# Chunked linear attention without POOL: one query product, copied by ScalarE into the block-diagonal tile; splits of the earliest norm on VectorE

## The chip, the core and the metric

The kernel runs on one core of a Trainium2 chip. The metric is the time of one execution on the device in microseconds (us), as the median of several runs. The engines are TensorE (PE in the profile; PEld is its weight load), VectorE (DVE), ScalarE (ACT), GpSimd (POOL) and SyncE (SP), which here only issues transfers.

## The reference

Two layers of a transformer block work on 512 latent tokens and 256 context tokens of width 1024. Each layer is: half a SwiGLU feed-forward step, a token mixer with three head groups (gated linear attention, windowed attention, differential attention) that share an input and an output projection, and a second half feed-forward step, all with modulated RMS norms. In the last layer the context tokens only serve as keys. The part that the change touches is the gated linear attention, in chunks, forwards and backwards:

```python
def step(state, inp):
    kc, vc, gc = inp[0], inp[1], inp[2]
    cum = jnp.cumsum(gc, axis=2)
    last = cum[:, :, -1:, :]
    new_state = (jnp.exp(last[:, :, 0, :, None]) * state
                 + jnp.einsum('bhjd,bhjv->bhdv', kc * jnp.exp(last - cum), vc))
    qc = inp[3]
    o_inter = jnp.einsum('bhid,bhdv->bhiv', qc * jnp.exp(cum), state)
    decay = jnp.exp(jnp.where(causal, cum[:, :, :, None, :] - cum[:, :, None, :, :], -jnp.inf))
    att = jnp.einsum('bhid,bhjd,bhijd->bhij', qc, kc, decay)
    return new_state, o_inter + jnp.einsum('bhij,bhjv->bhiv', att, vc)
```

All is float32; the kernel keeps that accuracy by splitting each operand of a large product into a high and a low part and adding three products.

## The kernel before

Activations lie transposed, features on the partitions and tokens along the columns. A large product is three TensorE instructions (`mm3`, lines 405 to 407). The high part of an operand is a rounded copy by ScalarE (`split`, line 369), the low part a subtraction on VectorE or POOL (line 370). Weights come in by transfers that SyncE issues.

`gla_mix` (line 1302) is the linear attention after its projections. For each direction it makes the cumulated log gates (lines 1334, 1336), the keys scaled to the end of each chunk (1346 to 1348), the states chunk by chunk (1361 to 1368) and the scaled queries for the states (1375, 1376). Within a chunk of 128 it doesn't form the decay for each pair of tokens, but goes through seven levels of block size s = 64, 32, 16, 8, 4, 2, 1. At each level and for each direction `d`, the queries of one half of a block of 2s tokens meet the keys of the other half. This takes, for one level-direction:

- line 1417: the cumulated gates minus those of the middle of each block, into `E` (128 partitions x n tokens);
- lines 1418, 1419: two exponentials of half of `E` each, on ScalarE;
- line 1423: the keys times their half of `E`;
- lines 1424 to 1427: for each of the four heads (32 partitions each) the queries times their half of `E`, written into the head's own columns of `qbd`, a tile that is zero elsewhere, so that one TensorE product yields all four heads apart (block-diagonal);
- lines 1439, 1444 or 1450: the TensorE products of keys and `qbd`;
- lines 1454 to 1469: the results go into the attention tile, by copies for s of 64 and 32, by predicated copies on VectorE for the rest.

`E`, `qbd` and the keys have three buffers each that rotate from one level-direction to the next. n is 512 for the latent tokens and 256 for the context; layer 0 does both, layer 1 the first alone, so there are 14 + 14 + 14 level-directions.

This work doesn't run alone. The tail of the windowed attention (lines 1198 to 1248), the output projection of the other two head groups (lines 405 to 407 with 1534, whose operands are split by lines 369 and 370) and the modulation of later stages (lines 274 to 331) are traced between its steps. The order of the instructions on each engine is fixed when the program is built, by a scheduler that may move an instruction ahead of earlier ones of the trace. An engine works through its queue in that order.

The table `CFG` (line 86) names the engine of each piece of work by a letter: V for VectorE, P for POOL, A for ScalarE. `GK` stands for lines 1348, 1376 and 1417, `KV` for line 1423, `Q` for the four heads of line 1427, `HS` for the low parts of the first feed-forward weights, that come in two halves (`half_split`, line 865, called at lines 1668 and following), `NA` for the norms: a letter per feature block, d for a fused low part on VectorE (line 461), s or S for a `split` of the finished value, whose low part is on POOL for s and on VectorE for S (line 458).

At the start, the norm of the first feed-forward step (`norm_x`, line 1660) is made in two halves of four feature blocks, as the modulation of each half is ready, and the first products of that step begin with the first half. Lines 711 to 729 (`t_prep`) then prepare sums of the normed blocks on VectorE for the later products.

Of the kernel before, what the change touches and what calls it, by code (L numbers as in the profile page):

```python
# [15 lines left out]
ALU = mybir.AluOpType  # L16
# [66 lines left out]
    return rope, mats, masks  # L83


CFG = dict(big=('VVVV', 'PPPP', 'VVVV', 'VVVV', 'VV'), small=('VPVV', 'PPPP', 'VVVV', 'VVPP', 'VV'), T=['VVVVVVVVVVVV', 'VVVVVVVVVVVV', 'VVVVVVVVVVVV', 'VVVVVVVVVVVV'], QW=['PVVV', 'VVVV', 'VVVV', 'VVVV'], QS=['VVVV', 'VVVV', 'VVVV', 'VVVV'], TS1=[0, 4, 0, 0], TS2=[0, 4, 0, 0], NA=['dsdsdsds', 'dsdsdsds', 'dsdsdsds', 'dsdsdsds', 'dsdsdsds', 'dsdsdsds'], RS='V', PS=['V', 'V', 'V', 'V'], PL=['V', 'V', 'V', 'V'], ORD='1c6u2eA5dxA37yfAg4hA', ORD1='1c236ueA5dxgA7yfA4hA', ORD2='1c236ueA5dxgA7yfA4hA', SPLIT=0.9, E0=18, E1=16, SA=10, SB=3, F0=(2, 14), F1=(0, 6), Q='PVVV', KV='P', OL='V', DM='sbsbsbsb', G3=2, N0=0, QB='bbbs', HS=['PPPP', 'PPPP'], LO='VV', RM='V', GK='PPP', DC='AAVV', SC='VAVAV', VE='AA', GC='VVA', ST='qxdrmlsnMSN', XS='AVAVAV', XE='VAVAVAVAVAVA', PB=['s', 'bb', 's', 'bb'])


@with_exitstack
def hybrid_kernel(ctx: ExitStack, tc: tile.TileContext, x, c, ctx_in, c_ctx, w_mod, b_mod, g_ffn1, w_ffn1_in,  # L90
# [3 lines left out]
    nc = tc.nc  # L94
# [8 lines left out]
    P = cpool.tile([128, 3840], F32, name="P")  # L103
# [47 lines left out]
    ENG = {"P": nc.gpsimd, "V": nc.vector}  # L151
# [15 lines left out]
    def copy(e, dst, src):  # L167
        if e == "A":
            nc.scalar.activation(dst, src, AF.Copy)
        else:  # L170
            ENG[e].tensor_copy(dst, src)
# [75 lines left out]
    def sum_x(a):  # L247

        sq = P[:, (a % 3) * 1024:(a % 3 + 1) * 1024]
        if CFG["XS"][a] == "V":  # L250
            nc.vector.scalar_tensor_tensor(sq, xin[a], 1.0, xin[a], op0=ALU.mult, op1=ALU.mult, accum_out=ss0[:, a:a + 1])
# [3 lines left out]
    def load_x():  # L255
        bank = cyc(gtile, atile, btile_, atile, stile, stile)

        for k in range(NK):
            ps = bank()
            for a in range(4):  # L260
                nc.tensor.transpose(ps[:, a * 128:(a + 1) * 128], xin[a][:, k * 128:(k + 1) * 128], ident)
            copy(CFG["XE"][k], xT[:, k, :SEQ], ps[:, :SEQ])
        for k in range(0, NK, 2):
            ps = bank()
            for b in range(4):
                nc.tensor.transpose(ps[:, b * 128:(b + 1) * 128], xin[4 + b % 2][:, (k + b // 2) * 128:(k + b // 2 + 1) * 128], ident)
            copy(CFG["XE"][NK + k // 2], xT[:, k:k + 2, SEQ:], ps[:, :512].rearrange("p (k t) -> p k t", k=2))

# [174 lines left out]
    def norm_apply(l, which, piece, pb, ks):  # L443
# [4 lines left out]
        for k in ks:  # L448
# [4 lines left out]
            sh = mod[l][:, si, k, t:t + 1]  # L453
            mode = CFG["NA"][3 * l + which][k]
            if mode in "sS":
# [65 lines left out]
    def ffn(l, which, w_i, w_o, pieces, side=None):  # L521
# [3 lines left out]
        beside = side() if side else iter(())  # L525
        ME, LE, WE, SE, UE = CFG["big" if pieces[-1][1] > SEQ else "small"]
        last = ((0, 256), (256, 512), CP) if CP in pieces else pieces
# [20 lines left out]
        def quad_stages(first=False):  # L548
            we, se = (CFG["QW"][fi], CFG["QS"][fi]) if first else (WE, SE)

# [751 lines left out]
    def gla_mix(l, cq):  # L1302
# [38 lines left out]
        for d in range(2):  # L1341
# [17 lines left out]
            for i, cc in enumerate(order):  # L1359
# [3 lines left out]
                for h in range(4):  # L1363
                    pr, vs = slice(32 * h, 32 * h + 32), slice(64 * h, 64 * h + 64)
# [16 lines left out]
        for t0, t1 in ((XP, CP) if cq else (XP,)):  # L1381
# [6 lines left out]
            for hf in range(2):  # L1388
                m = n // 2
                qbd = qbd_reg[rr[0] % 3].rearrange("p (h t) -> p h t", h=4)[:, :, :m]  # L1390
                rr[0] += 1
                for h in range(4):
                    pr = slice(32 * h, 32 * h + 32)
# [11 lines left out]
            for li, s in enumerate(LEVELS):  # L1405
                nb = n // (2 * s)
                ops = []
                for d in range(2):
                    cu = cum[d][:, t0:t1].rearrange("p (b t) -> p b t", t=2 * s)
                    mid = cu[:, :, s - 1:s] if d == 0 else cu[:, :, s:s + 1]  # L1410
                    E = e_reg[rr[0] % 3][:, :n].rearrange("p (b t) -> p b t", t=2 * s)
                    qbd = qbd_reg[rr[0] % 3].rearrange("p (h t) -> p h t", h=4)[:, :, :n // 2]
                    kt_ = kt_reg[rr[0] % 3][:, :n]
                    rr[0] += 1
                    iq = slice(s, 2 * s) if d == 0 else slice(0, s)
                    jk = slice(0, s) if d == 0 else slice(s, 2 * s)
                    ENG[CFG["GK"][2]].tensor_tensor(E, cu, mid.to_broadcast([128, nb, 2 * s]), op=ALU.subtract)
                    act(E[:, :, iq], E[:, :, iq], AF.Exp, scale=TAU)
                    act(E[:, :, jk], E[:, :, jk], AF.Exp, scale=-TAU)
                    q3 = g_q[:, t0:t1].rearrange("p (b t) -> p b t", t=2 * s)  # L1420
                    k3 = g_k[:, t0:t1].rearrange("p (b t) -> p b t", t=2 * s)
                    kv3 = kt_.rearrange("p (b t) -> p b t", t=2 * s)
                    ENG[CFG["KV"]].tensor_tensor(kv3[:, :, jk], k3[:, :, jk], E[:, :, jk], op=ALU.mult)
                    for h in range(4):
                        pr = slice(32 * h, 32 * h + 32)
                        eng = ENG[CFG["Q"][h]]
                        eng.tensor_tensor(qbd[pr, h].rearrange("p (b t) -> p b t", t=s), q3[pr, :, iq], E[pr, :, iq], op=ALU.mult)
                    ops.append((qbd, kt_))
                for r0 in (range(0, ncn, 2) if s == 64 else (0,)):
                    rn = 2 if s == 64 else ncn  # L1430
                    pl = btile()
                    for d in range(2):
                        qbd, kt_ = ops[d]
                        for cc in range(r0, r0 + rn):
                            kc = kt_[:, cc * 128:(cc + 1) * 128]
                            cl = cc - r0
                            if s == 64:
                                po = 64 * d
                                nc.tensor.matmul(pl[po:po + 64, cl * 256:(cl + 1) * 256], kc[:, po:po + 64],
                                                 qbd[:, :, cc * 64:(cc + 1) * 64], start=True, stop=True)  # L1440
                            elif s == 32:
                                for b in range(2):
                                    po = 64 * b + 32 * d
                                    nc.tensor.matmul(pl[po:po + 32, cc * 128:(cc + 1) * 128], kc[:, po:po + 32],
                                                     qbd[:, :, cc * 64 + 32 * b:cc * 64 + 32 * b + 32],
                                                     start=True, stop=True)
                            else:
                                co = d * n // 2 + cc * 64
                                for g in range(4):
                                    nc.tensor.matmul(pl[32 * g:32 * g + 32, co:co + 64], kc[:, 32 * g:32 * g + 32],  # L1450
                                                     qbd[:, :, cc * 64 + 16 * g:cc * 64 + 16 * g + 16], start=True, stop=True)
                    if s == 64:
                        p4 = pl[:, :rn * 256].rearrange("p (c h i) -> p c h i", c=rn, h=4)
                        nc.scalar.copy(att[0:64, r0:r0 + rn, :, 64:128], p4[0:64])
                        nc.vector.tensor_copy(att[64:128, r0:r0 + rn, :, 0:64], p4[64:128])
                    elif s == 32:
                        p4 = pl[:, :n].rearrange("p (c h i) -> p c h i", c=ncn, h=4)
                        for g in range(4):
                            pr = slice(32 * g, 32 * g + 32)
                            io = 32 * (g ^ 1)  # L1460
                            (nc.scalar.copy if g % 2 else nc.vector.tensor_copy)(att[pr, :, :, io:io + 32], p4[pr])
                    else:
                        for d in range(2):
                            io = s if d == 0 else 0
                            a = li - 2
                            mk = masks[:, (5 * d + a) * 16:(5 * d + a + 1) * 16]
                            src = pl[:, d * n // 2:(d + 1) * n // 2]
                            dst = dg.rearrange("p c h i -> p (c h) i").rearrange("p a (b t) -> p a b t", t=2 * s)[:, :, :, io:io + s]
                            nc.vector.copy_predicated(
                                dst, mk.rearrange("p (b t) -> p b t", t=s).unsqueeze(1).to_broadcast([128, ncn * 4, 16 // s, s]),  # L1470
                                src.rearrange("p (a b t) -> p a b t", b=16 // s, t=s))
                yield
            for g in range(4):
                pr = slice(32 * g, 32 * g + 32)
# [26 lines left out]
    SPLIT = CFG["SPLIT"]  # L1501
# [116 lines left out]
    G3 = CFG["G3"]  # L1618
# [147 lines left out]
```

## Time and profile before

| | |
|---|---|
| runs, us | 2964.78, 2964.88, 2969.39; median 2964.88 |
| profiled execution, us | 2966.68 |
| its span, first to last instruction, us | 2964.9 |
| granted TensorE clock, mean | 0.991 |
| PE busy, us | 2857.1 |
| DVE busy, us | 2215.8 |
| ACT busy, us | 1222.6 |
| POOL busy, us | 455.5 |

The busy times are sums over instructions of one engine; engines run side by side, so they don't add up to the span. A line of the profile names the source line of the instruction (L1427), its engine, its operation, the tile written and the tiles read, the shape as partitions x columns, and the number of instructions. A share of the clock of 1.00 is 2.4 GHz, half of it 1.2 GHz. The tile names H, W1, W2, FA, FB, A2, G, B and so on are areas that hold different things at different stages; f or r behind them is the type.

### The profile page before, as it was taken

How to read it: one execution, taken by the hardware profiler on the slowest of the kernel's cores; microseconds unless marked ns; L12 is line 12 of the kernel's file. 1: busy time of each engine (PE TensorE's matmuls, PEld its weight loads, DVE VectorE, ACT ScalarE, POOL GpSimd, SP SyncE). 2: the span in 40 equal slices, each digit the busy share in tenths (PEclk: the TensorE clock that was granted, in tenths of full speed). 3: DMA queues.
4: the chain of work that ended last, by engine and by line, in shares of the span. 5: the costliest groups of instructions: out<-in, count | busy, mean ns of one | idle time of the engine just before them, and what ended most of it. 6: DMA issues, size and time to landing. Idle time of an engine off the chain costs nothing. (4 is left out here: it accounts for less than half of the span.)

```text
span 2964.9 us, 48602 instructions
## 1 busy us (share of the span) xinstructions
PE 2857.1 (96%) x19464; PEld 2499.0 (84%) x19464; DVE 2215.8 (75%) x3925; ACT 1222.6 (41%) x2310; POOL 455.5 (15%) x440
## 2 busy tenths in 40 slices
PE   7899999999999889999999999999999999899998
PEld 5798999888776568999999899999988766689898
DVE  6777787655668878878776787777664678799996
ACT  4333333345455435333333542333354555354443
POOL 3001011110002431101010101101010013123432
PEclk9999999999999999999999999999999999999999
DMA  6332312223445341221212122212222343223332
GB/s 219 114 121 86 93 58 88 68 54 92 100 127 171 101 128 30 85 71 57 86 58 72 44 72 70 73 60 69 72 66 70 77 134 100 72 79 116 91 106 87
DMA packets 314245, 262.38 MB, mean 88 GB/s; under 512 B 27528, under 2 KB 290340, under 8 KB 314020
## 3 DMA queue, kind: packets, MB, share of 16 engines
q1 hardware_dynamic: 311712, 255.47, 29.1%
q10 hardware_dynamic: 2308, 3.82, 0.4%
q8 instruction: 153, 2.51, 0.3%
q14 instruction: 72, 0.59, 0.1%
HBM read 247.72 MB, written 2.10 MB: 84 GB/s over the span
## 5 line engine op out<-in xcount | busy, mean ns | idle before, releaser
L369 ACT ACTIVATE W0r<-R 128x1024 fp32r<-128x1024 f32 (+2 forms) x229 | 219.6, 965 | 353.5 <-PE a L407 78.3
L370 DVE TENSOR_TENSOR W0r<-R,W0r 128x1024 fp32r<-128x1024 f32 (+1 forms) x193 | 215.8, 1123 | 61.8 <-ACT W0r L369 37.4
L369 ACT ACTIVATE W1r<-R 128x1024 fp32r<-128x1024 f32 (+1 forms) x149 | 141.7, 953 | 250.1 <-PE a L406 74.5
L825 DVE SCALAR_TENSOR_TENSOR X<-s,dmod,X 128x512 f32<-128x512 f32 x252 | 150.5, 627 | 65.9 <-PE s L407 65.9
L370 POOL TENSOR_TENSOR FAr<-P,FAr 128x384 fp32r<-128x384 f32 (+1 forms) x64 | 75.7, 1187 | 566.8 <-ACT FAr L369 533.9
L370 POOL TENSOR_TENSOR FBr<-P,FBr 128x384 fp32r<-128x384 f32 (+1 forms) x60 | 72.4, 1208 | 582.2 <-ACT FBr L369 480.9
L405 PE MATMUL g<-Hr,W0r 128*128 128x384 f32 (+3 forms) x400 | 140.3, 351 | 9.5 <-ACT P L163 9.3
L163 ACT ACTIVATE P<-s,sm 128x768 f32<-128x768 f32 (+3 forms) x160 | 119.0, 750 | 60.4 <-DVE sm L1061 38.5
L406 PE MATMUL g<-Hr,W0r 128*128 128x384 f32 (+3 forms) x400 | 136.7, 342 | 0.2 <-POOL Hr L370 0.2
L370 DVE TENSOR_TENSOR W1r<-R,W1r 128x1024 fp32r<-128x1024 f32 (+1 forms) x102 | 109.3, 1078 | 26.3 <-ACT W1r L369 12.8
L825 DVE SCALAR_TENSOR_TENSOR X<-a,dmod,X 128x256 f32<-128x256 f32 (+1 forms) x170 | 101.9, 600 | 30.4 <-PE a L407 30.2
L407 PE MATMUL g<-Hr,W0r 128*128 128x512 f32 (+3 forms) x324 | 112.4, 347 | 1.1 <-DVE W0r L370 1.1
L556 DVE TENSOR_TENSOR P<-R 128x512 f32<-128x512 f32 x80 | 58.0, 725 | 65.2 <-DMA R<-in_w_ffn_in_dram 65.2
L407 PE MATMUL a<-Hr,W0r 128*128 128x384 f32 (+2 forms) x332 | 106.7, 321 | 0.0
L1061 DVE TENSOR_REDUCE sm<-s 128x1 f32<-128x768 f32 (+1 forms) x80 | 65.8, 844 | 41.3 <-PE s L1060 41.2
L405 PEld LDWEIGHTS g<-Hr,W0r 128*128 128x128 f32 (+1 forms) x400 | 74.4, 186 | 23.8 <-ACT P L163 9.5
L370 POOL TENSOR_TENSOR Hr<-P,Hr 128x256 fp32r<-128x256 f32 (+1 forms) x64 | 55.1, 862 | 254.4 <-ACT Hr L369 253.6
L405 PE MATMUL a<-Hr,W0r 128*128 128x384 f32 (+2 forms) x280 | 91.8, 328 | 0.4 <-DVE ms L330 0.4
L406 PE MATMUL a<-Hr,W0r 128*128 128x384 f32 (+2 forms) x280 | 90.9, 325 | 0.0
L369 ACT ACTIVATE FAr<-P 128x384 fp32r<-128x384 f32 (+2 forms) x80 | 39.8, 498 | 113.2 <-DVE P L769 83.5
L405 PE MATMUL s<-Hr,W0r 128*128 128x384 f32 (+2 forms) x240 | 81.5, 340 | 5.0 <-ACT Hr L460 4.8
L405 PE MATMUL b<-Hr,W0r 128*128 128x384 f32 (+3 forms) x248 | 82.8, 334 | 1.0 <-DVE sm L1208 0.5
(853 smaller groups left out, 10167.9 us busy)
## 6 DMA issues: line engine op xcount, KB each, us to landing
R<-in_w_ffn_in_dram SPq DMA_DIRECT2D x164, 512.0 KB, 4.4
R<-in_w_mod_dram SPq DMA_DIRECT2D x104, 512.0 KB, 4.4
R<-in_w_ffn_out_dram SPq DMA_DIRECT2D x40, 1024.0 KB, 4.9
R<-in_w_in_dram SPq DMA_DIRECT2D x28, 512.0 KB, 4.0
W2f<-in_w_mod_dram SPq DMA_DIRECT2D x24, 512.0 KB, 3.6
R<-in_w_ffn_in_dram SPq DMA_DIRECT2D x6, 1024.0 KB, 5.1
Gr<-Bf SPq DMA_DIRECT2D x48, 96.0 KB, 2.2
Hf<-in_w_mod_dram SPq DMA_DIRECT2D x4, 1024.0 KB, 13.4
```

Source lines behind the costliest of these rows:

```text
L163: i = nc.scalar.activation(dst, src, func, **kw).ins
L369: nc.scalar.activation(dst_hi, src, AF.Copy)
L370: (lo_eng or nc.vector).tensor_tensor(dst_lo, src, dst_hi.bitcast(F32), op=ALU.subtract)
L405: nc.tensor.matmul(ps, wh, rh, start=first, stop=False)
L406: nc.tensor.matmul(ps, wh, rl, start=False, stop=False)
L407: nc.tensor.matmul(ps, wl, rh, start=False, stop=last)
L556: ENG[se[0]].tensor_tensor(SB[:, 0:512], a21, a22, op=ALU.add)
L825: nc.vector.scalar_tensor_tensor(xT[:, m, p0:p1], p_, dmod[l][:, 3 + which, m, t:t + 1], xT[:, m, p0:p1], op0=ALU.mult, op1=ALU.add)
L1061: nc.vector.tensor_reduce(sm[:, s:s + 1], S[:, k0:TOK], AX.X, ALU.max, negate=True)
```

## The change

The four per-head query products of each level-direction become one product over all 128 partitions, in place in `E`, on VectorE. Its four parts are then copied into the block-diagonal tile, by ScalarE for all four heads (`QC='AAAA'`). The subtraction of line 1417, the key products and the products of lines 1348 and 1376 go from POOL to VectorE. So do the low parts of the first weights (`HS`, two times four splits of 128x512) and those of the odd feature blocks of the very first norm (`NA[0]`: four blocks of 512 and four of 256 tokens). The zero fills of lines 1378 and 1379 stay on POOL, and so does POOL's work elsewhere.

```diff
-CFG = dict(..., NA=['dsdsdsds', 'dsdsdsds', ...], ..., Q='PVVV', KV='P', ..., HS=['PPPP', 'PPPP'], ..., GK='PPP', ...)
+CFG = dict(..., NA=['dSdSdSdS', 'dsdsdsds', ...], ..., QC='AAAA', KV='V', ..., HS=['VVVV', 'VVVV'], ..., GK='VVV', ...)
@@ -1421,10 +1421,10 @@
                     k3 = g_k[:, t0:t1].rearrange("p (b t) -> p b t", t=2 * s)
                     kv3 = kt_.rearrange("p (b t) -> p b t", t=2 * s)
                     ENG[CFG["KV"]].tensor_tensor(kv3[:, :, jk], k3[:, :, jk], E[:, :, jk], op=ALU.mult)
+                    nc.vector.tensor_tensor(E[:, :, iq], q3[:, :, iq], E[:, :, iq], op=ALU.mult)
                     for h in range(4):
                         pr = slice(32 * h, 32 * h + 32)
-                        eng = ENG[CFG["Q"][h]]
-                        eng.tensor_tensor(qbd[pr, h].rearrange("p (b t) -> p b t", t=s), q3[pr, :, iq], E[pr, :, iq], op=ALU.mult)
+                        copy(CFG["QC"][h], qbd[pr, h].rearrange("p (b t) -> p b t", t=s), E[pr, :, iq])
                     ops.append((qbd, kt_))
```

## Rows read from the trace of the kernel before

**Rows 1.** The page, busy us, share of the span and instructions of an engine.
```profile
PE 2857.1 (96%) x19464; PEld 2499.0 (84%) x19464; DVE 2215.8 (75%) x3925; ACT 1222.6 (41%) x2310; POOL 455.5 (15%) x440
```
**Rows 2.** Busy us by stretch; columns: length, PE, PEld, DVE, ACT, POOL, clock, DMA.
```profile
890.00:910.00 20.00, 15.86 (x136) 9.45 (x133) 17.24 (x38) 13.21 (x37) 11.24 (x12) 0.91 0.44 136
960.00:1030.00 70.00, 57.00 (x760) 39.01 (x758) 64.37 (x134) 34.90 (x85) 33.30 (x35) 0.98 0.37 114
1040.00:1090.00 50.00, 42.06 (x443) 28.37 (x440) 40.28 (x95) 16.51 (x49) 24.49 (x42) 0.97 0.37 109
2480.00:2550.00 70.00, 55.92 (x698) 38.57 (x696) 64.61 (x115) 28.54 (x64) 32.21 (x35) 0.93 0.35 95
sum 210.00, PE 170.84 PEld 115.40 DVE 186.50 ACT 93.17 POOL 101.24; mean PE 42.71 PEld 28.85 DVE 46.63 ACT 23.29 POOL 25.31
```
**Rows 3.** Waits of PE, whole span: who waited for whom, us, times, longest.
```profile
PE g L1450 <- DVE Hf L1427: 10.9, 6, 3.2
...
PE s L1450 <- DVE Hf L1427: 2.6, 3, 1.4
...
PE g L1450 <- POOL FBf L1417: 1.7, 1, 1.7
```
**Rows 4.** Timeline of DVE: start us, us, line, shape, count (merged where back to back).
```profile
906.65 1.75 DVE L1204 SCALAR_TENSOR_TENSOR sm<-sm,nsink 128x2 f32<-128x2 f32 x1
...
986.55 1.28 DVE L1427 TENSOR_TENSOR Hf<-W1f,Hf 32x256 f32<-32x256 f32 x3
...
1001.95 4.31 DVE L1427 TENSOR_TENSOR Hf<-W1f,Hf 32x256 f32<-32x256 f32 x3
```
**Rows 5.** Groups of DVE, shapes apart, line 1427: count, busy us, mean ns, idle before.
```profile
L1427 DVE TENSOR_TENSOR Hf<-W1f,Hf 32x256 f32<-32x256 f32 x54 | 38.4, 712 | 2.2 <-PE g L1399 0.7 <-ACT Hf L163 0.3
L1427 DVE TENSOR_TENSOR FBf<-W1f,FBf 32x256 f32<-32x256 f32 x30 | 17.4, 580 | 1.0 <-ACT FBf L163 0.3
L1427 DVE TENSOR_TENSOR Hf<-W1f,Hf 32x128 f32<-32x128 f32 x30 | 12.2, 407 | 2.0 <-ACT Hf L163 1.4
L1427 DVE TENSOR_TENSOR FBf<-W1f,FBf 32x128 f32<-32x128 f32 x12 | 5.5, 459 | 0.3
```
**Rows 6.** Groups of DVE, two-input instructions little disturbed; last, one of the timeline.
```profile
L1496 DVE TENSOR_TENSOR Hf<-Hf,s 128x512 f32<-128x512 f32 x4 | 2.7, 687 | 4.1 <-PE s L985 4.1
...
L1248 DVE TENSOR_TENSOR FAf<-FAf,a 128x256 f32<-128x256 f32 x4 | 1.6, 410 | 0.5 <-PE a L1244 0.5
...
L1330 DVE TENSOR_TENSOR Hf<-Hf 128x768 f32<-128x768 f32 x4 | 3.8, 950 | 0.0
...
1058.09 0.28 DVE L1427 TENSOR_TENSOR Hf<-W1f,Hf 32x128 f32<-32x128 f32 x1
```
**Rows 7.** Groups of ACT, shapes apart: block-diagonal copies of line 1394, exponentials.
```profile
L163 ACT ACTIVATE Hf<-Hf 128x256 f32<-128x256 f32 x36 | 13.3, 415 | 28.6 <-POOL Hf L1417 28.6
...
L1394 ACT ACTIVATE Hf<-W1f 32x256 f32<-32x256 f32 x16 | 6.6, 411 | 1.2 <-POOL Hf L1378 1.0
...
L1394 ACT ACTIVATE Hf<-W1f 32x128 f32<-32x128 f32 x4 | 1.2, 308 | 0.7 <-PE s L1450 0.6
```
**Rows 8.** Timeline of PE: one kind of product, before and inside the slow clock.
```profile
2505.38 0.40 PE L407 MATMUL a<-A2r,W0r 128*128 128x512 f32 x1
...
2513.97 0.63 PE L407 MATMUL a<-A2r,W0r 128*128 128x512 f32 x1
```
**Rows 9.** Timelines of DVE and PE at the start of the kernel.
```profile
35.58 2.94 DVE L450 SCALAR_TENSOR_TENSOR P<-X,dmod,KLf 128x256 f32<-128x256 f32 x2
...
38.45 1.75 DVE L461 SCALAR_TENSOR_TENSOR Hr<-P,mod,Hr 128x512 fp32r<-128x512 f32 x1
...
50.65 0.69 DVE L284 TENSOR_TENSOR Bf<-Bf,a 128x512 f32<-128x512 f32 x1 [5.04 <-PE a L274]
...
57.69 3.75 DVE L450 SCALAR_TENSOR_TENSOR P<-X,dmod,KLf 128x256 f32<-128x256 f32 x4
...
87.83 0.69 PE L405 MATMUL g<-Hr,W0r 128*128 128x384 f32 x1 [9.29 <-ACT P L163]
```

More of the change, by code (lines that the diff above doesn't have):

```diff
@@ L83, in _shape_constants @@
     return rope, mats, masks
-CFG = dict(big=('VVVV', 'PPPP', 'VVVV', 'VVVV', 'VV'), small=('VPVV', 'PPPP', 'VVVV', 'VVPP', 'VV'), T=['VVVVVVVVVVVV', 'VVVVVVVVVVVV', 'VVVVVVVVVVVV', 'VVVVVVVVVVVV'], QW=['PVVV', 'VVVV', 'VVVV', 'VVVV'], QS=['VVVV', 'VVVV', 'VVVV', 'VVVV'], TS1=[0, 4, 0, 0], TS2=[0, 4, 0, 0], NA=['dsdsdsds', 'dsdsdsds', 'dsdsdsds', 'dsdsdsds', 'dsdsdsds', 'dsdsdsds'], RS='V', PS=['V', 'V', 'V', 'V'], PL=['V', 'V', 'V', 'V'], ORD='1c6u2eA5dxA37yfAg4hA', ORD1='1c236ueA5dxgA7yfA4hA', ORD2='1c236ueA5dxgA7yfA4hA', SPLIT=0.9, E0=18, E1=16, SA=10, SB=3, F0=(2, 14), F1=(0, 6), Q='PVVV', KV='P', OL='V', DM='sbsbsbsb', G3=2, N0=0, QB='bbbs', HS=['PPPP', 'PPPP'], LO='VV', RM='V', GK='PPP', DC='AAVV', SC='VAVAV', VE='AA', GC='VVA', ST='qxdrmlsnMSN', XS='AVAVAV', XE='VAVAVAVAVAVA', PB=['s', 'bb', 's', 'bb'])
+CFG = dict(big=('VVVV', 'PPPP', 'VVVV', 'VVVV', 'VV'), small=('VPVV', 'PPPP', 'VVVV', 'VVPP', 'VV'), T=['VVVVVVVVVVVV', 'VVVVVVVVVVVV', 'VVVVVVVVVVVV', 'VVVVVVVVVVVV'], QW=['PVVV', 'VVVV', 'VVVV', 'VVVV'], QS=['VVVV', 'VVVV', 'VVVV', 'VVVV'], TS1=[0, 4, 0, 0], TS2=[0, 4, 0, 0], NA=['dSdSdSdS', 'dsdsdsds', 'dsdsdsds', 'dsdsdsds', 'dsdsdsds', 'dsdsdsds'], RS='V', PS=['V', 'V', 'V', 'V'], PL=['V', 'V', 'V', 'V'], ORD='1c6u2eA5dxA37yfAg4hA', ORD1='1c236ueA5dxgA7yfA4hA', ORD2='1c236ueA5dxgA7yfA4hA', SPLIT=0.9, E0=18, E1=16, SA=10, SB=3, F0=(2, 14), F1=(0, 6), QC='AAAA', KV='V', OL='V', DM='sbsbsbsb', G3=2, N0=0, QB='bbbs', HS=['VVVV', 'VVVV'], LO='VV', RM='V', GK='VVV', DC='AAVV', SC='VAVAV', VE='AA', GC='VVA', ST='qxdrmlsnMSN', XS='AVAVAV', XE='VAVAVAVAVAVA', PB=['s', 'bb', 's', 'bb'])
 @with_exitstack
```

## The prediction, made before the change was run

> **What bounds the kernel now.** I read the page first: TensorE holds 96% of the span, VectorE 75% [rows 1]. A kernel so full can only gain where TensorE stands still, so the next view is busy time by stretch. Four stretches hold all the linear-attention work that the change touches: 890 to 910 us and 960 to 1030 us (layer 0, the 512 latent tokens), 1040 to 1090 us (layer 0, the 256 context tokens), 2480 to 2550 us (layer 1). Of their 210 us TensorE is busy 170.8, idle 39.2; VectorE is busy 186.5, and in the second and fourth about 92% of the time; ScalarE is busy 93.2, less than half; POOL 101.2 [rows 2]. So in these stretches, and in few others, VectorE is the engine that sets the pace.
>
> Who ends TensorE's waits says the same: the products of line 1427 on VectorE and the POOL subtraction of line 1417 end 15.2 us of them in the three longest groups [rows 3]; the rest is spread over many short waits on other VectorE work in the same queue.
>
> Third, what makes VectorE so busy. Three of its 32x256 products take 1.28 us when POOL does nothing, and 4.31 us while POOL runs its own share of the same level; a 128x2 product, that has next to nothing to do, took 1.75 us beside POOL's 128x768 product [rows 4]. The two engines disturb each other, so a VectorE instruction can cost over three times its price while POOL is busy.
>
> **The change, part by part.** I make the sum against the profiled execution, 2966.68 us with a span of 2964.9; the median of the three runs, 2964.88, is 1.8 us lower, and the last step takes that off.
>
> Linear attention on VectorE. There are 28 level-directions of 512 tokens (14 in each layer) and 14 of 256. Before, each gives VectorE three products of 32 partitions: 126 in all, 73.5 us [rows 5]. Alone they would take 84 x 0.43 (a third of the 1.28 us in rows 4) and 42 x 0.28 [rows 6], together 47.9 us, so some 26 us of it is stretch from POOL. After, each direction gives VectorE a subtraction, a key product and a query product over 128 partitions: 0.69 + 0.41 + 0.41 us at 512 tokens, 0.41 + 0.28 + 0.28 at 256 [rows 6] (a product costs by its columns, not by its partitions, so the 32x128 row stands for 128x128). That is 28 x 1.51 + 14 x 0.97 = 55.9 us. Line 1348 adds four products of 128x768 and line 1376 two of 128x768 and two of 128x512: 6 x 0.95 + 2 x 0.69 = 7.1 us [rows 6]. VectorE so gives up 73.5 and takes 63.0: 10.5 us less, although it does all of POOL's work. The other VectorE instructions of these stretches (186.5 - 73.5 = 113 us) lose their stretch too. I can't see how much; I put it at 10 us, a stretch of 9% where line 1427 had over 50%, with ends at 0 and 26. VectorE is then relieved of 20.5 us (10.5 to 36).
>
> How much of that TensorE sees: 39.2 us of idle time is there to be had, and VectorE is nearly the only candidate in two of the four stretches, less so in the context stretch where it is busy 40.3 of 50 us. I take two thirds of the relief: **14 us less**, with ends at 0 (another engine is late in its place) and 30.
>
> The query copies on ScalarE. 28 x 4 copies of 32x256 at 0.41 us and 14 x 4 of 32x128 at 0.31 [rows 7] (line 1394 does this very kind of copy into the same tile) are 63.3 us more on ScalarE. Its cover is its own idle time, 210 - 93.2 = 117 us in these stretches, and the exponentials of the 512-token levels alone wait 28.6 us for POOL's subtraction [rows 7]. With the copies it stands at 156 of 210 us. I cost them at nothing; without that cover they cost up to 63.3 us. They bring one new wait: a copy must wait until TensorE has read its block-diagonal buffer three directions before, a wait that VectorE and POOL had. Behind it on ScalarE stand the next direction's exponentials, the weight and activation splits of line 369 for the output projection, and PSUM evacuations, and TensorE waits for all of these. The chain of one direction gets no shorter by itself: 0.69 (subtract) + 0.83 (two exponentials) + 0.41 (product) + 1.64 (four copies) = 3.6 us after; before, the last two steps were 3 x 0.43 = 1.3 us undisturbed, and 4.3 us as the third of rows 4. The gain is the stretch, not fewer steps.
>
> TensorE's clock. The granted clock was 0.91, 0.98, 0.97 and 0.93 in the four stretches [rows 2]: after gaps TensorE is held at 1.2 GHz for a while, where a 128x512 product takes 0.63 us and not 0.40 [rows 8]. The means lose 1.8 + 1.4 + 1.5 + 4.9 = 9.6 us of full clock. Fewer gaps give part back: **2 us less**, ends 0 and 6.
>
> The earliest norm and the first weight splits. Eight 128x512 weight splits and four 128x512 plus four 128x256 norm splits go to VectorE: 12 x 0.69 + 4 x 0.41 = 9.9 us. Four of the weight splits fall where VectorE idles 5.04 us before line 284 [rows 9] and cost nothing. The other 7.1 us lie on a queue that the timeline shows packed up to 91 us, and whose end ends the 9.29 us wait of TensorE at 87.8 us (through ScalarE's SiLU, which stands behind splits of VectorE's sums in its queue) [rows 9]. Against them the stretch goes: two 128x256 products that took 2.94 us, one 128x512 that took 1.75 and four 128x256 that took 3.75 should take 0.82, 0.69 and 1.64 [rows 6, 9], 5.3 us less, and there are smaller ones. I take **1 us more**, ends -1 and +7. If a split of a weight is late, TensorE's third product of that k waits for it (line 407), and all behind it.
>
> POOL keeps the feed-forward splits and the norm splits of the later layers, so all else stays as it is. The scheduler orders each engine's queue anew when instructions change engine, which may move a few us anywhere; I add 3 us to both ends for it.
>
> **The sum**: 2966.7 - 14 - 2 + 1 = 2951.7, and 1.8 less on the scale of the median: about 2950.
>
> **The rivals.**
> (a) *Turned into another wait.* The chain per direction stays at 3.6 us, the copies wait for TensorE, and TensorE's waits end on ScalarE where they ended on VectorE. For: the 15.2 us of rows 3 all hang on that chain. Against: VectorE's own queue, not the chain, is full in two of the four stretches. Relief of 0 to 3 us, time 2959 to 2970, say 2964.
> (b) *ScalarE becomes the bound: slower.* Per level of 512 tokens it has eight copies (3.3 us), four exponentials (1.66 us) and its evacuations, over 5 us in one queue in order, while the swa exponentials and line 369 stand in the same queue. It decides once more than 15 of the 63.3 us, a quarter, stand ahead of something that TensorE waits for; if a half does, the time is 2965 + 32 - 15 = 2982. Against: ScalarE's 117 us of idle time. The Trainium skill ("ScalarE: Activation LUTs", Rules for kernel authors) sends plain elementwise work to VectorE and not to ScalarE; by that rule this rival would be the outcome, and no run so far shows it.
> (c) *More than forecast.* If POOL and VectorE exclude each other for whole instructions, VectorE gets back far more than I put down, up to the 36 us end, and the idle of 39.2 us all but goes: 30 us for the gaps and 4 for the clock, 2965 - 34 = 2931. The rows with 4.31 and 1.75 us speak for it; that many stretched instructions are only slightly stretched speaks against. The Trainium skill ("SBUF — State Buffer", SBUF: two separate sides) says just this: a shared port pair is locked for the whole instruction between a VectorE instruction with two SBUF inputs and a GpSimd one that reads SBUF. By that rule, the trace agrees in rows 4.
> (d) *The head loses.* Rows 9 come out at their bad end, +7, and a new order costs 3 more elsewhere, with the main part as forecast: 2956 to 2960. I count it into the forecast's range.
>
> **How the numbers follow.** Forecast (2940 to 2959): 0.57. (c): 0.10. (a): 0.20. (b): 0.13. A measurement of this kernel can't tell less than 0.2%, 5.9 us, from no change. Faster by more: 0.57 + 0.10 - 0.02 for (d) = 0.65. Within it: 0.20 for (a), 0.02 for (d) and 0.02 of (b) at its mild end, 0.24. Slower: the other 0.11 of (b). The range holds the forecast, all of (a), the mild end of (b) and, with its lower end, half of (c): 2934 to 2970.
>
> **What would show it.** In the changed profile: line 1417 on VectorE at about 0.69 us for 128x512, its query product at 0.41; VectorE's busy time in the four stretches lower by about 20 us though it has more instructions; ScalarE there at about 150 us; TensorE's idle time in them from 39 to about 25 us and its clock nearer 1. The waits of lines 1439, 1444 and 1450 should end on ScalarE's copies and be shorter in sum. The forecast is wrong if ScalarE's queue shows exponentials waiting behind copies while TensorE waits for them, if VectorE's instructions keep their stretch without POOL, or if the wait at 88 us grows by more than 3 us.

## The result and the profile after

| | before | after |
|---|---|---|
| runs, median us | 2964.83 | 2936.70 (2932.32 to 2939.21) |
| ratio, 95% interval | | 0.9905 [0.9893, 0.9917] |
| profiled span, us | 2964.9 | 2937.4 |

The change makes the kernel 28 us faster (25 to 32). The forecast was 15 us, 2950, with a range of 2934 to 2970. The measured 2936.7 is inside that range, near its lower end, and below the 2940 to 2959 that the prediction gave the forecast itself.

The page of after, busy us by engine, answers [rows 1]:

```profile
PE 2857.1 (97%) x19464; PEld 2498.2 (85%) x19464; DVE 2179.3 (74%) x3949; ACT 1284.9 (44%) x2478; POOL 319.8 (11%) x290
```

TensorE's busy time is the same to the tenth. So the whole gain is time in which TensorE stood still: 107.8 us of the span before, 80.3 after.

Where it stood still is seen in three wide windows around the linear attention. They are wider than [rows 2], since the same work now lies some us earlier. First before, then after; columns: length, PE, PEld, DVE, ACT, POOL, clock, DMA:

```profile
880.00:920.00 40.00, 35.57 (x307) 21.53 (x306) 33.41 (x90) 24.11 (x59) 12.50 (x12) 0.96 0.51 159
920.00:1100.00 180.00, 158.76 (x1755) 110.41 (x1754) 147.09 (x358) 78.42 (x202) 60.72 (x79) 0.98 0.42 130
2450.00:2580.00 130.00, 113.61 (x1211) 84.03 (x1210) 107.16 (x228) 56.49 (x127) 34.98 (x37) 0.96 0.32 94
sum 350.00, PE 307.94 PEld 215.97 DVE 287.65 ACT 159.02 POOL 108.19; mean PE 102.65 PEld 71.99 DVE 95.89 ACT 53.01 POOL 36.06
```

```profile
880.00:920.00 40.00, 36.49 (x319) 23.20 (x318) 34.24 (x98) 24.91 (x62) 1.48 (x2) 1.00 0.60 189
920.00:1100.00 180.00, 169.02 (x1824) 120.76 (x1825) 130.25 (x363) 119.28 (x319) 0.95 (x1) 0.97 0.43 130
2450.00:2580.00 130.00, 124.57 (x1262) 93.51 (x1261) 98.02 (x226) 89.50 (x203) 4.49 (x6) 0.99 0.34 97
sum 350.00, PE 330.08 PEld 237.46 DVE 262.51 ACT 233.69 POOL 6.92; mean PE 110.03 PEld 79.15 DVE 87.50 ACT 77.90 POOL 2.31
```

TensorE's idle time falls from 42.1 to 19.9 us. ScalarE carries 75 us more in them, POOL 101 us less, and VectorE, which took over most of POOL's part, is busy 25 us less.

The waits of TensorE in the levels, whole span of after, answer [rows 3]; columns: who waited for whom, us, times, longest:

```profile
PE g L1450 <- ACT Hf L169: 2.7, 2, 2.2
PE g L1450 <- ACT FBf L169: 1.8, 2, 1.1
PE s L1450 <- ACT Hf L169: 0.6, 3, 0.2
```

They end on ScalarE's copies (line 169 is the helper of line 1427 of after) where they ended on line 1427 and POOL. These are the three largest groups in the levels, 5.1 us. The prediction's 15.2 us were not quite the three longest, since two groups of 1.8 us stand before the last of them, 1.7, but the sum changes by 0.1 us only.

A second measure is of use below: the first or last start of a line marks a stage. After, line 1399 first starts at 959.7 us and the output products of line 1490 at 1019.8:

```profile
L1399 PE MATMUL g<-Hf,W1f x72: 272/273/297, 959.7 to 2469.5; 128*32 128x128 f32 x72
L1490 PE MATMUL g<-Hf,W1f x32: 272/273/324, 1019.8 to 1031.1; 128*64 128x128 f32 x32
```

So the seven levels of the latent tokens took 60.1 us. The same, read from the traces of before, after and of the runs below, in us. The first column is the first start of line 1334. The latent levels run from the first start of line 1399 to the first of line 1490. The context column runs from there to the first start of line 1490 for the context tokens, so it holds the output products of the latent tokens too. The levels of layer 1 run from the last start of line 1399 to the last of line 1490. The last column is the sum of the three.

| kernel | 1334 at | latent levels, layer 0 | context levels | levels, layer 1 | sum |
|---|---|---|---|---|---|
| before | 889.5 | 64.0 | 58.5 | 76.3 | 198.8 |
| after | 885.1 | 60.1 | 52.1 | 67.1 | 179.3 |
| e1, start alone | 879.5 | 64.4 | 58.4 | 75.5 | 198.3 |
| e2, attention alone | 891.1 | 58.8 | 52.2 | 67.2 | 178.2 |
| e3, four products | 885.7 | 70.0 | 59.0 | 81.4 | 210.4 |
| e4, copies on VectorE | 880.8 | 63.9 | 59.7 | 77.0 | 200.6 |
| e6, one copy on VectorE | 884.5 | 55.9 | 50.7 | 69.1 | 175.7 |
| e7, one copy on POOL | 881.2 | 58.1 | 49.3 | 66.5 | 173.9 |
| e11, two copies on POOL | 881.5 | 54.0 | 49.9 | 63.5 | 167.4 |
| e12, one on VectorE, one on POOL | 880.5 | 53.7 | 50.4 | 69.4 | 173.5 |

### The profile page after: what moved, and what is told of

The parts are those of the page before. It is cut to its first block, busy times and chain, and to the rows that moved or that the text cites. A ratio compares the mean times of both kernels' runs of the same rounds, so it can differ in the third digit from the quotient of the medians.

```text
span 2937.4 us, 48575 instructions
## 1 busy us (share of the span) xinstructions
PE 2857.1 (97%) x19464; PEld 2498.2 (85%) x19464; DVE 2179.3 (74%) x3949; ACT 1284.9 (44%) x2478; POOL 319.8 (11%) x290
## 5 line engine op out<-in xcount | busy, mean ns | idle before, releaser
L825 DVE SCALAR_TENSOR_TENSOR X<-s,dmod,X 128x512 f32<-128x512 f32 x252 | 150.6, 628 | 67.1 <-PE s L407 67.1
L370 POOL TENSOR_TENSOR Hr<-P,Hr 128x256 fp32r<-128x256 f32 x56 | 45.5, 813 | 444.6 <-ACT Hr L369 443.7
L405 PE MATMUL s<-Hr,W0r 128*128 128x384 f32 (+2 forms) x240 | 81.4, 339 | 5.0 <-ACT Hr L460 4.8
## 6 DMA issues: line engine op xcount, KB each, us to landing
Hf<-in_w_mod_dram SPq DMA_DIRECT2D x4, 1024.0 KB, 14.2
```

Of the source, the lines that this page charges most:

```text
L370: (lo_eng or nc.vector).tensor_tensor(dst_lo, src, dst_hi.bitcast(F32), op=ALU.subtract)
L405: nc.tensor.matmul(ps, wh, rh, start=first, stop=False)
L825: nc.vector.scalar_tensor_tensor(xT[:, m, p0:p1], p_, dmod[l][:, 3 + which, m, t:t + 1], xT[:, m, p0:p1], op0=ALU.mult, op1=ALU.add)
```

## The experiments

Each ratio is against the kernel before on the same chip. "us" is the ratio less one, times 2964, with its interval. A difference between two experiments is a difference of these "us" values. Each run also has a new order of every engine's queue, and no run shows what that alone is worth, so a difference of a few us within the intervals is not put down to anything.

| run | median | ratio | us |
|---|---|---|---|
| after | 2936.70 | 0.9905 | -28.2 (-31.7 to -24.6) |
| e1 start alone | 2957.61 | 0.9981 | -5.6 (-8.3 to -3.0) |
| e2 attention alone | 2944.22 | 0.9940 | -17.8 (-21.6 to -14.2) |
| e3 four products on VectorE | 2966.75 | 1.0010 | +3.0 (+0.3 to +5.6) |
| e4 copies on VectorE | 2956.44 | 0.9973 | -8.0 (-10.7 to -5.0) |
| e5 first norm alone | 2957.24 | 0.9981 | -5.6 (-8.0 to -3.0) |
| e6 copies AAAV | 2932.17 | 0.9896 | -30.8 (-35.3 to -26.4) |
| e7 copies AAAP | 2928.97 | 0.9886 | -33.8 (-37.6 to -29.6) |
| e8 subtraction on POOL | 2941.10 | 0.9926 | -21.9 (-25.5 to -18.1) |
| e9 company, two inputs | 2938.51 | 0.9921 | -23.4 (-27.6 to -19.6) |
| e10 company, one input | 2939.95 | 0.9919 | -24.0 (-27.9 to -19.9) |
| e11 copies AAPP | 2923.74 | 0.9868 | -39.1 (-43.3 to -35.3) |
| e12 copies AAVP | 2926.56 | 0.9876 | -36.8 (-40.9 to -32.9) |

**The two parts.** e1 is before with the start of after:

```diff
-NA=['dsdsdsds', ...], HS=['PPPP', 'PPPP']
+NA=['dSdSdSdS', ...], HS=['VVVV', 'VVVV']
```

> Only the part at the start: the low parts of the first weights and of the odd blocks of the first norm on VectorE, the linear attention as before. The forecast's step put this part at +1 us (2966). The trace after has 2.2 us more TensorE work in the first 150 us than the trace before, so a second theory says about 2 us faster (2962). If the order that the scheduler makes in the whole rest is what matters, neither holds and it moves by more than 4 us either way.

e2 is after with the start of before (the same diff the other way round).

> Only the linear attention is changed, the start as before. Theory 1, all of the main gain is from the four stretches: TensorE idles 42.1 us before and 19.9 us after in the windows around them, so 22 us faster, 2942 to 2944. Theory 2, the parts help each other or the start gives more than its windows show: less than 18 us faster, above 2947. Together with the run of the head alone the two gains should add up to the 28 us of the whole.

The start alone gives 5.6 us, more than either theory's number by the median. Its expectation puts a move of more than 4 us down to the order of the whole rest. The profiles don't bear that out: of the 11.2 us between the spans of before and e1, 10.0 are there when line 1334 first starts, ahead of the levels, though that mark scatters by some us (last section). The attention alone gives 17.8, between the two theories of e2: 2944.2 is just above the first one's 2944, and 17.8 just under the second one's 18. Together the parts make 23.4, and the 28.2 of the whole lie within the intervals of the two; the 4.8 us between are not explained. The page of e1 tells what happened at the start:

```profile
PE 2850.0 (96%) x19464; PEld 2493.8 (84%) x19464; DVE 2215.3 (75%) x3941; ACT 1223.7 (41%) x2310; POOL 435.1 (15%) x424
```

VectorE got splits that the prediction put at 9.9 us, yet it is busy 0.5 us less than before [rows 1]: 10.4 us of stretch went.

**Which half of the start.** e5 moves the first norm alone:

```diff
-NA=['dsdsdsds', ...]
+NA=['dSdSdSdS', ...]
```

> Only the low parts of the odd blocks of the first norm go to VectorE; the first weights' splits stay on POOL and the linear attention is as before. Head alone (both) came out at 2957.6. Theory 1, POOL's 1.6 us low parts of the norm were what TensorE and VectorE's stretch hung on: 2956 to 2960. Theory 2, the weight splits on POOL, 1.4 us each at 30 to 40 us, were what stretched VectorE's first blocks: little changes here, 2962 to 2966.

It gives all of e1's 5.6 us: theory 1. The weight splits' move neither gives nor costs anything that these runs can tell. The timeline of VectorE in e5 against [rows 9]: as long as POOL still makes the weight splits, the two products of line 450 keep their stretch, but those beside the norm's old low parts lose it.

```profile
34.88 2.92 DVE L450 SCALAR_TENSOR_TENSOR P<-X,dmod,KLf 128x256 f32<-128x256 f32 x2
37.72 0.74 DVE L461 SCALAR_TENSOR_TENSOR Hr<-P,mod,Hr 128x512 fp32r<-128x512 f32 x1
...
60.00 0.87 DVE L450 SCALAR_TENSOR_TENSOR P<-X,dmod,KLf 128x256 f32<-128x256 f32 x2
```

The 2.92 us stand as they stood (2.94); 1.75 us became 0.74, and two of the four products that took 3.75 take 0.87.

**No POOL, but the old products.** e3 is after with the loop of before, all heads on VectorE:

```diff
-nc.vector.tensor_tensor(E[:, :, iq], q3[:, :, iq], E[:, :, iq], op=ALU.mult)
 for h in range(4):
-    copy(CFG["QC"][h], qbd[pr, h].rearrange(...), E[pr, :, iq])
+    eng = ENG[CFG["Q"][h]]          # Q='VVVV'
+    eng.tensor_tensor(qbd[pr, h].rearrange(...), q3[pr, :, iq], E[pr, :, iq], op=ALU.mult)
```

> As after, but the four products per head of before, all on VectorE, in place of one product and four copies on ScalarE; POOL does nothing in the levels. VectorE gets 28 x (4 x 0.43 - 0.42) + 14 x (4 x 0.28 - 0.28) = 48 us more than after, ScalarE 63 us less. Theory 1 (POOL beside VectorE was the cost, and it is gone here too): most of the gain stays, 2938 to 2948. Theory 2 (VectorE's load is the bound, and ScalarE's taking of the products is what gives the gain): VectorE had some 40 us idle in the 200 us of the stretches, so it is full, and the gain is gone: 2960 to 2985.

e4 is after with the copies on VectorE:

```diff
-QC='AAAA'
+QC='VVVV'
```

> As after, but the four copies into the block-diagonal tile on VectorE. The Trainium skill (ScalarE: Activation LUTs, Rules for kernel authors) sends plain copies to VectorE. Theory by that rule: ScalarE is 92 to 99 per cent busy in the 512-token levels after the change, so taking 63 us off it makes it faster, 2925 to 2935, if the copies cost VectorE 0.25 us each or less. Rival (VectorE's load is the bound): at 0.43 and 0.28 us each VectorE gets 28 x 1.7 + 14 x 1.1 = 63 us more, is full, and the time is 2965 to 2995.

e3 has no POOL in the levels, and all that the change should have gained there is gone: 8.6 us slower than e1, which has the attention of before and the same start. Its page, its three windows together, and its products:

```profile
PE 2871.4 (97%) x19464; PEld 2509.6 (85%) x19464; DVE 2227.4 (75%) x4075; ACT 1222.9 (41%) x2310; POOL 320.1 (11%) x290
...
sum 350.00, PE 311.51 PEld 216.80 DVE 297.04 ACT 154.78 POOL 3.38; mean PE 103.84 PEld 72.27 DVE 99.01 ACT 51.59 POOL 1.13
...
L1427 DVE TENSOR_TENSOR Hf<-W1f,Hf 32x256 f32<-32x256 f32 x72 | 29.9, 415 | 1.8 <-PE g L1399 0.9
```

VectorE, no longer disturbed, is busy 12 us more than in e1: the stretch that it gets back only pays for POOL's work. The loss shows twice: for the same instructions TensorE is busy 14.3 us more than in after (2871.4 against 2857.1), at a mean granted clock of 0.986 against 0.993, and that is nearly half of the 32.2 us by which the span is longer; the rest is idle time. One product and four copies on VectorE (e4) take 11.0 us off e3, because there a copy is cheap:

```profile
L171 DVE COPY Hf<-Hf 32x256 f32<-32x256 f32 x72 | 20.4, 283 | 1.5 <-PE g L1399 0.7
```

That is 283 ns against 415 for a product of this shape. The same copies on ScalarE cost 420 ns each, and yet the kernel, after, is 20.2 us faster with them there:

```profile
L169 ACT ACTIVATE Hf<-Hf 32x256 f32<-32x256 f32 x72 | 30.2, 420 | 4.9 <-DVE Hf L1424 3.0 <-PE g L1399 0.9
```

So theory 2 of e3 held, with its numbers. In e4 the theory by the rule fell (2925 to 2935 was written), although its condition of 0.25 us a copy was nearly met: 283 and 216 ns, 0.26 us in the mean. Its rival held in direction, at a milder size. This speaks for VectorE's load and against the length of one direction's chain: the last two steps of the chain, product and copies or four products, take 2.10 us in after (0.42 + 4 x 0.42), 1.66 in e3 (4 x 0.415) and 1.55 in e4 (0.42 + 4 x 0.283), and the two shorter chains are slower.

The Trainium skill ("ScalarE: Activation LUTs", Rules for kernel authors) sends `relu`, `max`, `min`, `add` and `mul` to VectorE as the faster engine. Copies are not in that row; the expectation of e4 carried it over to them. The price agrees in direction (283 against 420 ns), but the choice that follows from it does not, since here VectorE was the full engine.

**Is ScalarE the bound now?** e6, e7, e11 and e12 take copies off ScalarE again:

```diff
-QC='AAAA'
+QC='AAAV'     # e6;  'AAAP' e7;  'AAPP' e11;  'AAVP' e12
```

> As after, but the fourth head's copy on VectorE, which the run with all copies there shows to take 0.28 us for 32x256 and 0.22 for 32x128 against 0.42 and 0.31 on ScalarE. VectorE gets 28 x 0.28 + 14 x 0.22 = 11 us more, ScalarE 16 us less. Theory 1, VectorE's load is the bound (four copies there cost 20 us): 4 to 6 us slower than after, 2941 to 2943. Theory 2, ScalarE, 92 to 99 per cent busy in the 512-token levels of after, has become the bound: 2 to 6 us faster, 2931 to 2935.

> As after, but the fourth head's copy on POOL. It loads neither VectorE nor ScalarE (16 us less there). Theory 1, contention: POOL beside VectorE stretches VectorE as before, and its copy, perhaps 0.6 to 0.9 us, comes late: 2 to 10 us slower than after, 2939 to 2947. Theory 2, load alone counts: 1 to 5 us faster, 2932 to 2936.

> Copies of two heads on ScalarE, two on POOL. One copy on POOL gave 7.7 us. Theory 1, ScalarE's load is still what counts: another 16 us off it, 2 to 6 us faster than e7, 2923 to 2927. Theory 2, POOL's copies, 0.50 to 0.59 us each and two behind each other, are late in the chain: 0 to 5 us slower than e7, 2929 to 2934.

> Copies of two heads on ScalarE, one on VectorE, one on POOL. One of four on VectorE gave 4.5 us, one on POOL 7.7. Theory 1, the three engines' loads are what counts: ScalarE another 16 us less than in e7, VectorE 11 us more: 1 to 4 us faster than e7, 2925 to 2928. Theory 2, VectorE is the bound as soon as ScalarE is relieved: 1 to 5 us slower than e7, 2930 to 2934.

Taking copies off ScalarE helped in all four: they are faster than after by 2.6 (e6), 5.6 (e7, a little more than written), 10.9 (e11) and 8.6 us (e12). For e6 and e7 the intervals still overlap with after's, for e11 and e12 they do not. Even e6 is not slower, with VectorE busy 10.9 us more (2190.2), so VectorE's load no longer sets the pace alone. POOL looks the better place, but e7 against e6 and e11 against e12 lie within their intervals; what the pages show is that e7 leaves VectorE's busy time as it is (2179.2 us). e11 (2179.1) is the fastest kernel here, 1.3% under before. The stage table agrees: 5.4 us off the levels for one head on POOL, 11.9 for two, 3.6 in e6 and 5.8 in e12. These runs don't part two reasons: ScalarE has less to do, and the four copies, 1.69 us one after the other, become a shorter row, since another engine makes its copies at the same time. Where it shows is in the levels of the latent tokens, first in after, then in e11 (same columns as above):

```profile
980.00:990.00 10.00, 8.28 (x149) 5.53 (x143) 7.50 (x25) 9.84 (x22) 0.00 (x0) 0.83 0.47 151
990.00:1000.00 10.00, 5.93 (x99) 4.49 (x96) 7.65 (x17) 9.20 (x22) 0.00 (x0) 0.77 0.35 106
```

```profile
980.00:990.00 10.00, 7.89 (x107) 4.63 (x106) 8.92 (x23) 9.63 (x22) 2.14 (x4) 1.00 0.62 186
990.00:1000.00 10.00, 8.68 (x130) 6.03 (x131) 9.57 (x19) 7.04 (x18) 2.80 (x6) 1.00 0.40 133
```

In after ScalarE is busy 92 to 98 per cent of these 20 us, TensorE idles 5.8 of them, and its clock is granted at 0.83 and 0.77, some of it at the lower level, 1.2 GHz. What stands in ScalarE's queue there is seen in its timeline of after:

```profile
985.96 1.28 ACT L159 ACT_TABLE_LOAD   x1
987.25 1.58 ACT L163 ACTIVATE Bf<-Bf 128x768 f32<-128x768 f32 x2
988.85 1.28 ACT L159 ACT_TABLE_LOAD   x1
...
992.15 1.69 ACT L169 ACTIVATE Hf<-Hf 32x256 f32<-32x256 f32 x4 [0.67 <-DVE Hf L1424]
993.86 1.69 ACT L169 ACTIVATE FBf<-FBf 32x256 f32<-32x256 f32 x4
```

The SiLU of the attention's output gate with a table load on each side, 4.2 us, stands ahead of two level-directions' exponentials and copies, and TensorE's product at 993.89 us waits 2.18 us for the first four copies. What moving that SiLU would give was not tried. In e11 it stands in the queue as well, from 982.11 to 986.28 us, and TensorE's clock stays at 1.00. The page of e11, and what TensorE's waits in its levels end on:

```profile
PE 2846.3 (97%) x19464; PEld 2492.5 (85%) x19464; DVE 2179.1 (75%) x3949; ACT 1253.1 (43%) x2394; POOL 361.1 (12%) x374
...
PE g L1450 <- POOL Hf L171: 3.6, 5, 1.6
```

Of the 16.7 us between the spans of after and e11, 10.8 are in TensorE's busy time (2857.1 and 2846.3), the same instructions, in part at a higher clock (0.993 and 0.995 in the mean), and 5.9 in its idle time. The longest group of waits in the levels now ends on POOL's copies.

**Is POOL's company itself a cost?** e8 puts the subtraction back on POOL; e9 and e10 add to after a POOL instruction per level-direction whose result nobody reads:

```diff
-GK='VVV'
+GK='VVP'     # e8
```

```diff
+nc.gpsimd.tensor_tensor(reg["W2"][:, 512:512 + n], kt_, kt_, op=ALU.mult)     # e9
+nc.gpsimd.tensor_copy(reg["W2"][:, 512:512 + n], kt_)     # e10, in its place
 ops.append((qbd, kt_))
```

> As after, but the subtraction of the gates (line 1417) on POOL, as before. VectorE gets 28 x 0.69 + 14 x 0.42 = 25 us less, POOL 28 x 1.13 + 14 x 0.65 = 41 us. Theory 1, load alone: 5 to 12 us faster than after, 2925 to 2932. Theory 2, contention and the chain (0.45 us longer per direction, and the exponentials on ScalarE wait for POOL again): 3 to 12 us slower, 2940 to 2949.

> As after, plus one POOL product of two tiles in SBUF for each level-direction, of the keys with themselves into a free area, 28 of 128x512 and 14 of 128x256; nothing reads its result, so it adds no work to VectorE or ScalarE and stands in no chain. It is there only as POOL's company, about as much (41 us) as the subtraction was in e8. Theory 1, POOL beside VectorE has a price of its own: in e8 VectorE was relieved of 25 us of instructions but its busy time in the stretches fell by 9 only, so 16 us of stretch; at VectorE's price of 20 us for 44 us of load that is 5 to 9 us slower than after, 2942 to 2946. Theory 2, the stretch is harmless, and e8 lost by the longer chain: 2935 to 2939.

> The same with a POOL copy, one input, in place of the product of two. Theory 1, any POOL instruction that reads SBUF stretches VectorE: as e9, 2941 to 2946. Theory 2, only POOL's two-input instructions do, as in e7, where VectorE's query product stood at 432 ns beside POOL's copies against 420 in after: 2935 to 2939.

The groups of line 1417 (128x512) and of the query product on VectorE, first beside POOL's products (e9), then beside its copies (e10); alone they take 687 and 420 ns:

```profile
L1417 DVE TENSOR_TENSOR Hf<-Hf 128x512 f32<-128x512 f32 x18 | 15.0, 833 | 1.5 <-ACT Hf L169 1.5
...
L1424 DVE TENSOR_TENSOR Hf<-W1f,Hf 128x256 f32<-128x256 f32 x18 | 10.2, 564 | 0.4 <-ACT Hf L163 0.3
```

```profile
L1417 DVE TENSOR_TENSOR Hf<-Hf 128x512 f32<-128x512 f32 x18 | 12.8, 712 | 2.0 <-ACT Hf L169 1.8
...
L1424 DVE TENSOR_TENSOR Hf<-W1f,Hf 128x256 f32<-128x256 f32 x18 | 7.9, 438 | 1.1 <-ACT Hf L163 0.9
```

The pages of e9 and e10:

```profile
PE 2854.7 (97%) x19464; PEld 2495.7 (85%) x19464; DVE 2191.4 (75%) x3949; ACT 1285.0 (44%) x2478; POOL 360.2 (12%) x332
```

```profile
PE 2853.4 (97%) x19464; PEld 2494.4 (85%) x19464; DVE 2181.4 (74%) x3949; ACT 1284.5 (44%) x2478; POOL 345.4 (12%) x332
```

By these, 40.4 us of POOL products made VectorE busy for 12.1 us more (2191.4), 25.6 us of POOL copies for 2.1 us more (2181.4). In time e9 and e10 are 4.8 and 4.2 us slower than after, with intervals that overlap with after's and with each other. So the stretch is shown, and its price in time is between nothing and some 10 us: the theories of e9 aren't told apart, nor those of e10. e8 is 6.3 us slower than after, with intervals that just overlap, although VectorE has 25 us of instructions less; how much of that is company and how much the longer chain stays open as well.

## Why the prediction was right, and where it was not

**What bounds the kernel.** Right: TensorE's gaps in the four stretches, set by VectorE. Relative to e1, VectorE's busy time and the time move roughly together as long as ScalarE has room: e3 +12.1 and +8.6 us, e4 +4.2 and -2.4 (no clear change), after -36.0 and -22.6. From after to e3 that is 31.2 us for 48.1 us of load, 0.65.

**VectorE's relief.** Forecast 20.5 us (10.5 to 36), measured by the page of e2 (2179.3 against 2215.8): 36.5, just beyond the far end:

```profile
PE 2856.9 (97%) x19464; PEld 2497.1 (85%) x19464; DVE 2179.3 (74%) x3933; ACT 1285.0 (44%) x2478; POOL 339.9 (12%) x306
```

The 10.5 for the replaced instructions were sound, since their prices came out as taken: 0.415 and 0.282 us in e3 for the old ones undisturbed, and in after, for line 1417 and the query product:

```profile
L1417 DVE TENSOR_TENSOR Hf<-Hf 128x512 f32<-128x512 f32 x18 | 12.4, 687 | 2.4 <-ACT Hf L169 2.2
...
L1424 DVE TENSOR_TENSOR Hf<-W1f,Hf 128x256 f32<-128x256 f32 x18 | 7.5, 420 | 1.4 <-ACT Hf L163 1.3
```

The mis-sized term is the stretch of all other instructions, put at 10 us: 36.5 - 10.5 = 26 us. Example: the 128x2 operation of line 1204 has a mean of 250 ns before and 156 after.

**What TensorE sees of it.** Forecast two thirds and 2 us of clock, 16 of 20.5; measured 17.8 of 36.5, about half. Two errors of size cancelled: the sum of this part was right (-16 against -17.8) with both its factors off. That is luck, and not a sign that the steps were sound. The 2 us of clock do not show: TensorE's busy time is 2857.1 us before and 2856.9 in e2, and its mean granted clock 0.991 in both. That the copies were not free (next paragraph) is part of why the share is so small.

**ScalarE's copies at nothing.** Duration and sum were right (64.1 us; ScalarE 152.0 us in the four stretches, said 156). The price of nothing was wrong: e11 takes 32 us of them off ScalarE and leaves VectorE's load alone, and gains 10.9 us. The cover was counted over 210 us, but in 20 us of the latent levels of layer 0 there is hardly any to spare (92 to 98 per cent busy, above). Rival (b) thus came in part, inside a gain; as an outcome it is out.

**"The gain is the stretch, not fewer steps."** This sentence failed. In e3 all the stretch is gone and no gain is left. The stretch that goes (about 26 us on line 1427 and 26 on the rest) pays for taking POOL's work; the gain is 48 us of VectorE's time that 64 us of an emptier engine replace. Rival (c) named the right amount of relief (its 36 us end), and the mechanism that it names is seen in e9, but its time of 2931 needs TensorE to see all of it. Rival (a) is out: the waits did turn to ScalarE, at a third of their length.

**The start.** Forecast +1 (-1 to +7), measured -5.6 (-8.3 to -3.0): outside. The failed step is the tally of the stretch, 5.3 us against 10.4 by the page of e1; with it VectorE's net is -0.5 and not +4.6. That a weight split costs time on the packed queue is not borne out either (e5 against e1). The 9.29 us wait at 88 us fell to this in after:

```profile
85.71 0.45 PE L405 MATMUL g<-Hr,W0r 128*128 128x384 f32 x1 [1.41 <-ACT P L163]
```

It is the norm's move that goes with it: the wait stands in e2, with the start of before, and is short in e5, with the norm's move alone (first e2, then e5):

```profile
PE g L405 <- ACT P L163: 9.3, 1, 9.3
```

```profile
PE g L405 <- ACT P L163: 1.2, 1, 1.2
```

But 3.56 us for a transfer of modulation weights, at 79.83 us, and 1.77 us for a weight split stand beside it in after. How the start's gain divides between its waits, its clock and its order isn't settled.

**The signs.** In the same four stretches VectorE is busy 155.1 us, 31 less (about 20 was said), ScalarE 152.0 (about 150), and TensorE idles 16.8 us (about 25); the work lies earlier, in layer 1 by 18 us, so they do not hold quite the same. Of the signs of being wrong, one came in part: in after, at 995.58 us, the splits of line 369 stand on ScalarE behind eight copies, and TensorE waits 0.83 us for one of them. A wait of TensorE for exponentials behind copies is not seen there. TensorE's clock was to be nearer 1: it is, at 1.00, 0.93, 1.00 and 0.98 in the four stretches, but for the second, where the waits for ScalarE's full queue are. Rival (d) is out by the start's gain. So the range held, and the forecast's own band did not: the start was off by 6.6 us, the attention by 1.8, and 4.8 us of the whole belong to neither part.

## What to carry to other kernels

Ask of each engine how full it is in the stage, not how fast it is at the instruction: ScalarE was 48% dearer per copy than VectorE and still the right place, until it was full, and then two heads on POOL were right. Of several moves in one change, do each alone: here emptying POOL by itself lost, the split of the product into product and copies won once ScalarE took the copies, and the start was a change of its own. Count an engine's stretch by the busy time that the whole profile loses, not by the few rows where it is striking; the forecast's two tallies of it were 10 of 26 us and 5.3 of 10.4.

## What the runs showed of the hardware

- POOL's two-input instructions stretch VectorE's far more than its one-input copies: 12.1 us for 40.4 us of POOL's time against 2.1 for 25.6. The Trainium skill ("SBUF — State Buffer", SBUF: two separate sides) names an exclusive lock between a VectorE instruction with two SBUF inputs and any GpSimd one that reads SBUF; e9 agrees, while in e10 its effect is small. The 128x2 operation of [rows 4] agrees too: it ran from 906.65 to 908.40 us, and POOL's product beside it ended at 908.39:

```profile
906.58 1.81 POOL L1348 TENSOR_TENSOR Hf<-Hf,W1f 128x768 f32<-128x768 f32 x1 [1.77 <-ACT Hf L163]
```

- In e11 POOL's own copies of one head's 32x256 take about 0.53 us, and VectorE's product beside them 442 ns against 420:

```profile
L171 POOL COPY Hf<-Hf 32x256 f32<-32x256 f32 x36 | 19.0, 529 | 89.2 <-PE g L1399 50.0 <-DVE Hf L1424 35.3 <-PE g L1444 2.5
...
L1424 DVE TENSOR_TENSOR Hf<-W1f,Hf 128x256 f32<-128x256 f32 x18 | 7.9, 442 | 0.3
```

- VectorE copies a 32x256 part within SBUF in 283 ns, where its two-input product takes 415.
- The time to line 1334 scatters by 6 us between profiles of the same start (879.5 to 885.7 us in after, e1, e3, e4 and e6 to e12), so a few us of the start can't be read from one profile; the timed runs decide.
